# Block 2's modulation with transposed weights, multiplied and summed along the row on VectorE, and no TensorE product

## The chip, the cores and the metric

One core of a Trainium2 chip runs the whole program. The metric is the device time of one launch in microseconds (us), the median over the runs shown. TensorE is called PE below, VectorE DVE, ScalarE ACT and SyncE, which issues nearly all transfers here, SP.

## The reference, cut to what matters

Two transformer blocks run one after the other on 1024 tokens of width 1024. The first ends with an MLP, `h + square(relu(norm(h) @ up_w)) @ down_w`, with a hidden width of 4096. The second is modulated by two small vectors:

```python
mod = silu(c) @ w_ada + b_ada                  # [6*1024]
sh1, sc1, gt1, sh2, sc2, gt2 = split(mod, 6)
mod_c = silu(c_ctx) @ w_ada + b_ada
csh1, csc1, ... = split(mod_c, 6)
hc = rmsnorm(ctx, g_mix) * (1 + csc1) + csh1
h = rmsnorm(x, g_mix) * (1 + sc1) + sh1
...
x = x + gt1 * (mixed @ w_out)
h2 = rmsnorm(x, g_ffn) * (1 + sc2) + sh2
x = x + gt2 * expert_choice_ffn(h2, ...)
```

Only the first two of the six parts are needed for `c_ctx`. So 6144 + 2048 numbers are wanted, each a sum of 1024 products, from a weight matrix of 24 MB. None of them depends on block 1.

## The kernel before

Every large product is made of float32 operands split into a high and a low part: three `pe.matmul` (lines 140 to 142) replace one. Weights come in units of [128, 1024] by a transfer on SP's queue (line 124), ACT writes the high part (115), DVE the low part (116). Five places hold split units, and `wunits` asks for them 1500 instructions ahead of the program's order. The order on each engine is made by a scheduler from the program's order and from when it thinks operands are ready; each engine then runs its queue strictly in order. Memory is 33 places of 4 KB (`R`) and 9 of 2 KB (`T`) per partition; each holds one tile at a time, in program order.

The MLP (755 to 786) runs over nine chunks of the hidden width, of 2, 2 and then 4 blocks of 128 each. In a chunk, "up" makes for each block and each half of the tokens 24 matmuls into one of five PSUM banks (`pm`), ACT takes relu (763) and square (765), DVE writes the two parts of `uT` (767, 768). Then "down" makes 16 groups of matmuls, and DVE adds each to the running sum `acc` (782).

The modulation (722 to 749) is woven into chunks 1 to 6, two of twelve groups of 512 columns in each. At a group, four units of `w_ada` (512 KB each) come into one place, `R32`, one after the other. Each holds two rows-of-128 of the contraction, with the 1024 inputs of the sum on partitions and the 512 outputs along the row. DVE multiplies by the per-partition scalar `cs` (739) and adds the next ones on top (741), into `macc` in place `T4` (and `T5` for `c_ctx`, in the first four groups). The sum over the 128 partitions is a PE product with a column of ones (746). DVE adds the bias `ba`, loaded into `T6` (743), on one partition (748, `mrow` in `T7`), and the row is stored to `mod_d` in DRAM (749). The places T4 to T7 hold before that the tiles `hx` of the residual update `add_out` (622 to 626) at the end of block 1's cross attention. `cs` is one small Silu of ACT (726).

After the MLP, six of the eight rows come back from `mod_d` as columns of 8 floats per partition (803 to 807, `modc`; 1055 to 1058, `modc2`), and enter `to_fm` (210 to 212), `fm_one` (268) and the router's product (1061). Four rows are read back to all partitions (`row_bc`, 791). Block 2 takes place T8 for the table `rope` (833).

Of the kernel before, what the change touches and what calls it, by code (L numbers as in the profile page):

```python
# [34 lines left out]
def tile_kernel(ctx: ExitStack, tc: tile.TileContext, d, out, stop=None, dbg=None):  # L35
# [21 lines left out]
    # On-chip memory: 33 places of 4 KB (R), 9 of 2 KB (T), 3 raw weight units, 5 split  # L57
    # weight units (hi, lo); each place holds one tile at a time, in program order.
# [19 lines left out]
    def tiny(shape, role=None, ring=32):  # L78
        """small vectors: 32 shared places of 8 floats; larger ones in places of their role"""
        n = tn.get(role, 0)  # L80
        tn[role] = n + 1
        return sb.tile(shape, F32, tag=f"y{role or ''}{n % ring}", bufs=1, name=nm("y"))

# [12 lines left out]
    cvec = small[:, 140:156]  # L96
# [8 lines left out]
    def bcast(t, src, n):  # L105
        """t [128, n] <- a row, on every partition"""
        nc.sync.dma_start(t, bass.AP(tensor=src.tensor, offset=src.offset, ap=[[0, 128], [1, n]]))
        return t
# [18 lines left out]
    def wunits(src, i0, n, ahead=1500):  # L127
        """units i0..i0+n of a stream, each [128, 2 (hi, lo), 1024]"""
        res = []
        with tc.high_priority(offset=ahead):  # L130
            for u in range(i0, i0 + n):
                raw = raw_unit(src[u])
                w = sb.tile([128, 2, 1024], F32R, tag=f"W{w_ring[0]()}", bufs=1, name=nm("w"))
                split(w[:, 0, :], w[:, 1, :], raw)
                res.append(w)
        return res

    def mm3(out_, l, r, first, last):
        """l, r: (hi, lo) pairs; out += l.T @ r"""
# [4 lines left out]
    def tm_part(p, lhs, units, k0, first, last):  # L144
        """p[128 tok, 512] += act @ W rows; lhs(k) -> (hi, lo); units: [2k x 512] each, from k0"""
# [9 lines left out]
    def fm_block(p, unit, rhs, n=512):  # L155
        """p[128 m, n tok] = W block.T @ act; unit [8k x 128]"""
# [5 lines left out]
    def rsqrt_of(ss, scale, n=1, eps=EPS):  # L162
        """(ss*scale + eps)^-0.5"""
# [6 lines left out]
        # one Newton step  # L170
# [28 lines left out]
    def evac_split(hi, lo, p, gain=None, shift=None):  # L199
        """hi + lo = p * gain + shift, both per partition"""  # L200
# [16 lines left out]
    def to_fm(xs, regs, banks, name="hT", gain=None, shift=None):  # L217
        """4 token tiles [128 tok, len(regs)*128] -> tiles [128 feat, 2, 512 tok]"""
# [10 lines left out]
    def fm_pairs(xs, regs, banks, gain, shift=None):  # L229
        """2 token tiles -> 4 tiles [128 feat, 2 k, 2 (hi, lo), 256 tok]"""  # L230
# [22 lines left out]
    def fm_one(x, regs, banks, parts=(0, 1), res=None, gain=None, shift=None):  # L253
        """a token tile [128 tok, 1024] -> k -> (hi, lo) [128 feat, 128 tok]"""
# [24 lines left out]
    def tile_of(hT, t):  # L279
        """lhs function of token tile t for hT = {half: [k tiles]}"""  # L280
# [32 lines left out]
    # =========================================================  # L313
    # block 1, mixer
    # =========================================================
# [3 lines left out]
    hT = {}  # L319
# [9 lines left out]
    # positions -> sin, cos [128 tok, 8 tiles, 16]  # L329
# [14 lines left out]
    def turns(k, a, unit):  # L344
        """k <- round(a / (2*pi*unit)) * unit"""
# [24 lines left out]
    # ca, cb -> u  # L370
# [18 lines left out]
    # conv taps  # L389
# [10 lines left out]
    # rg -> silu(rg); q, k rotated  # L400
# [22 lines left out]
    # v  # L423
# [11 lines left out]
    # retention: products in float32, a head's rows apart from the others' by zeros  # L435
# [7 lines left out]
    def retention(t):  # L443
# [7 lines left out]
        # transposes of q0 q1 k0 k1  # L451
# [39 lines left out]
        # state  # L491
# [20 lines left out]
        # group norm  # L512
# [33 lines left out]
    # merged branches, feature-major  # L546
# [43 lines left out]
    # memory keys and values  # L590
# [23 lines left out]
    hxT = Ring([4, 5, 6, 7])  # L614

    def add_out(src, units_src, act_T, tiles, dst_d, name, hxr):
        """dst = src + act @ W for token tiles"""
# [29 lines left out]
    # =========================================================  # L647
    # block 1, cross attention
    # =========================================================
# [65 lines left out]
    # =========================================================  # L715
    # block 1, MLP
    # =========================================================
# [3 lines left out]
    # modulation rows of block 2  # L721
    mod_d = dram([8, 1024], "mod_d")
    ones = cst.tile([128, 1], F32, name="ones")
    dve.memset(ones, 1.0)
    cs = cst.tile([128, 16], F32, name="cs")
    act.activation(cs, cvec, AF.Silu)

    def mod_group(g):
        """512 columns of the modulation"""
        r0, sl = g // 2, slice((g % 2) * 512, (g % 2) * 512 + 512)  # L730
        srcs = [(0, r0)] + ([(8, 6 + r0)] if r0 < 2 else [])
        accs = [T(4 + i, [128, 512], name="macc") for i in range(len(srcs))]
        for c in range(4):
            raw = load(R(32, [128, 1024], name="wada"), d["w_ada"][g * 4 + c]).rearrange("p (j n) -> p j n", j=2)
            for j in range(2):
                k = 2 * c + j
                for (o, _), a in zip(srcs, accs):
                    if k == 0:
                        dve.tensor_scalar(a, raw[:, j, :], cs[:, o:o + 1], None, op0=OP.mult)
                    else:  # L740
                        dve.scalar_tensor_tensor(a, raw[:, j, :], cs[:, o + k:o + k + 1], a, op0=OP.mult, op1=OP.add)  # L741
        ba = T(6, [1, 512], name="ba")
        load(ba, bass.AP(tensor=d["b_ada"].tensor, offset=d["b_ada"].offset + g * 512, ap=[[512, 1], [1, 512]]))
        for (_, r), a in zip(srcs, accs):
            p = B(pt(), "mod")
            pe.matmul(p[:1, :], ones, a, start=True, stop=True)
            row = T(7, [1, 512], name="mrow")
            dve.tensor_add(row, p[:1, :], ba)
            store(mod_d[r:r + 1, sl], row)
# [5 lines left out]
    for ch, fbs in enumerate(MLP_CHUNKS):  # L755
# [28 lines left out]
        if 1 <= ch < 7:  # L784
            mod_group(2 * ch - 2)
            mod_group(2 * ch - 1)

    # =========================================================
    # block 2, mixer
    # =========================================================  # L790
    def row_bc(i, r):
        return bc(i, mod_d[r:r + 1, :])

    def gain_of(i, src, r, tmp):
        """g * (1 + scale)"""
# [6 lines left out]
    modc = cst.tile([128, 4, 8], F32, name="modc")  # L802
    for i, r in enumerate((1, 0, 7, 6)):
        load(modc[:, i, :], mod_d[r:r + 1, :].rearrange("o (k p) -> p (o k)", k=8))
    for i in (0, 2):
        dve.scalar_tensor_tensor(modc[:, i, :], modc[:, i, :], 1.0, g_mix, op0=OP.add, op1=OP.mult)
    a1, sh1, ca1, csh = (modc[:, i, :] for i in range(4))
# [27 lines left out]
    def rotate(dst, p, nh, t):  # L835
        """dst, p: [128, nh*64]; rotation of tile t"""
# [72 lines left out]
    # window attention  # L909
# [21 lines left out]
    def attention(t):  # L931
        qt = load(T(6, [128, 512], name="qt"), q_d[t])
        # per head, partitions: 64 of hi, 64 of lo
# [13 lines left out]
        # keys of the first head of a pair: context, window; of the second: window, context  # L947
        for kv in range(2):
            Pl = []
            for hp in range(2):  # L950
# [3 lines left out]
                for jj in range(2):  # L954
                    h = h0 + jj
                    # context keys end the first bank, window keys start the second
# [9 lines left out]
                    with tc.high_priority(offset=1000):  # L966
                        dve.tensor_reduce(mx, sc, axis=AX.X, op=OP.max)
                        # minus the largest of scores / 8 and sink
# [30 lines left out]
            # rows 0-63: hi part, rows 64-127: correction  # L999
# [10 lines left out]
    # gated short convolution, to DRAM  # L1010
# [39 lines left out]
    # affinities of token tile 4 h + j in columns 32 h.. of part j  # L1050
# [3 lines left out]
    # router on the rows before their norm: logits = rstd * (x @ (gain * w)) + shift @ w  # L1054
    modc2 = cst.tile([128, 2, 8], F32, name="modc2")
    for i, r in enumerate((4, 3)):
        load(modc2[:, i, :], mod_d[r:r + 1, :].rearrange("o (k p) -> p (o k)", k=8))
    dve.scalar_tensor_tensor(modc2[:, 0, :], modc2[:, 0, :], 1.0, g_ffn, op0=OP.add, op1=OP.mult)
    p = B(7, "lb")
    for k in range(8):  # L1060
        pe.matmul(p[:, :16], modc2[:, 1, k:k + 1].to_broadcast([128, 128]), wr[:, k, :], start=(k == 0), stop=(k == 7))
    lbias = cst.tile([128, 16], F32, name="lbias")
    act.activation(lbias, p[:, :16], AF.Copy)
    dve.tensor_mul(wr, wr, modc2[:, 0, :, None].to_broadcast([128, 8, 16]))
# [7 lines left out]
    def mixed(half):  # L1072
        """x += gate * (mixed @ w_out), rows for the experts, affinities"""
# [54 lines left out]
    # =========================================================  # L1128
    # block 2, expert choice
    # =========================================================  # L1130
    # the 128 largest per expert of each half, descending (partitions 0.. and 32..)
# [24 lines left out]
    # slot i: the larger of A[i] and B[127 - i]  # L1156
# [60 lines left out]
    # the last expert's rows by a product with their one-hot matrix, then the norm  # L1217
# [23 lines left out]
def _tm(W, cols):  # L1241
    """column blocks of 512 -> units [128, (2k, 512)]"""
# [16 lines left out]
def _colp(v):  # L1259
    """[n*128] -> [128, n]"""  # L1260
# [37 lines left out]
def layout(inputs):  # L1298
# [8 lines left out]
    small[:, 140:148] = _colp(f["c_2"][0])  # L1307
    small[:, 148:156] = _colp(f["c_ctx_2"])
# [13 lines left out]
    a["b_ada"] = f["b_ada_2"][0]  # L1322
# [15 lines left out]
    # w_ada: 12 column groups x 4 x (2 k)  # L1338
    wa = f["w_ada_2"][0].reshape(4, 2, 128, 12, 512)
    a["w_ada"] = np.ascontiguousarray(np.transpose(wa, (3, 0, 2, 1, 4)).reshape(48, 128, 1024))  # L1340
# [35 lines left out]
```

## Time and profile before

| what | value |
|---|---|
| median of 3 runs | 2591.68 us (2587.64 to 2592.8) |
| span of the profiled execution | 2593.5 us |
| PE busy in the span | 2453.3 us (95%) |
| DVE busy | 1807.0 us (70%) |
| ACT busy | 1155.4 us (45%) |
[...]

The profiled execution is none of the three timed ones. Its span of 2593.5 us, from the first to the last instruction, is the only time given for it, and no time around it is shown. A busy PE is not PE at its peak, since matmuls overlap; what counts is whether it stands idle.

### The profile page before, as it was taken

Reading aid. Unit: us, or ns where it says so; the run is one execution under the profiler, and the core shown is the slowest. Engines: PE = TensorE matmul, PEld = TensorE weight load, DVE = VectorE, ACT = ScalarE, POOL = GpSimd, SP = SyncE. Lnnn points to the kernel's source line nnn. Section 1 sums busy time; section 2 is a strip of 40 time slices with the busy share of each in tenths; the row PEclk is TensorE's granted clock in tenths of the full one; section 3 lists DMA queues with packets and bytes.
Section 4 is the critical chain, followed back from the end, with each engine's and each line's share of the span. In section 5 each row is a group of like instructions: output and inputs, shape, how many; then the busy total and the mean of one; then the engine's idle time right before and its main releaser. Section 6 shows DMA issues by size and latency. Waiting matters only on the chain.

```text
span 2593.5 us, 31426 instructions
## 1 busy us (share of the span) xinstructions
PE 2453.3 (95%) x11504; PEld 1973.3 (76%) x11504; DVE 1807.0 (70%) x3091; ACT 1155.4 (45%) x1773; POOL 54.6 (2%) x35
## 2 busy tenths in 40 slices
PE   7999899999999999999999999999982999999996
PEld 6887678887877877887788777777772888888774
DVE  6999883655566454444434858776557999999888
ACT  6113552545432122112113725554331888887775
POOL 0000000000000000000000000000000100011100
PEclk9999999999999999999999999999995999999998
DMA  5233545334432233223211221114673999999994
GB/s 190 86 122 118 169 165 195 128 108 150 148 121 89 80 94 112 82 82 114 81 49 65 101 83 49 37 54 153 210 280 103 385 394 389 389 388 387 356 355 146
DMA packets 144003, 441.31 MB, mean 170 GB/s; under 512 B 21708, under 2 KB 26316, under 8 KB 143848
## 3 DMA queue, kind: packets, MB, share of 16 engines
q1 hardware_dynamic: 139384, 423.05, 46.1%
q0 software_dynamic: 4464, 16.25, 2.6%
q8 instruction: 90, 1.47, 0.2%
q14 instruction: 65, 0.53, 0.1%
HBM read 387.31 MB, written 51.94 MB: 169 GB/s over the span
## 4 chain that ended last, share of the span: by engine, by line
PE 75%; DVE 11%; DMA 9%; ACT 3%; issue 2%; SPq 0%; ACTq 0%; DVEq 0%; POOLq 0%
PE dn L141 6%; PE dn L142 6%; PE dn L140 6%; PE up L140 5%; PE up L141 5%; PE up L142 5%; DMA h_d<-hx 2%; PE ga L141 2%; PE ga L142 2%; PE wo L140 2%; PE wo L141 2%; PE wo L142 2%; PE ga L140 2%; DMA wada<-w_ada 2%; DVE w L116 2%
## 5 line engine op out<-in xcount | busy, mean ns | idle before, releaser
L115 ACT ACTIVATE w<-raw 128x1024 fp32r<-128x1024 f32 x560 | 584.3, 1058 | 767.6 <-PE dn L142 288.9
L116 DVE TENSOR_TENSOR w<-raw,w 128x1024 fp32r<-128x1024 f32 x560 | 673.7, 1222 | 182.9 <-ACT w L115 177.1
L782 DVE TENSOR_TENSOR acc<-dn,acc 128x512 f32<-128x512 f32 x144 | 98.7, 689 | 154.1 <-PE dn L142 153.9
L140 PE MATMUL up<-hm,w 128*128 128x512 f32 x512 | 201.7, 394 | 0.0
L141 PE MATMUL up<-hm,w 128*128 128x512 f32 x512 | 200.1, 391 | 0.0
L142 PE MATMUL up<-hm,w 128*128 128x512 f32 x512 | 199.9, 390 | 0.0
L140 PE MATMUL dn<-w,uT 128*128 128x512 f32 x512 | 199.4, 389 | 0.1
L141 PE MATMUL dn<-w,uT 128*128 128x512 f32 x512 | 199.2, 389 | 0.0
L142 PE MATMUL dn<-w,uT 128*128 128x512 f32 x512 | 199.0, 389 | 0.0
L396 DVE SCALAR_TENSOR_TENSOR y<-u,small,y 128x1015 f32<-128x1015 f32 (+26 forms) x120 | 146.3, 1262 | 0.6
L140 PEld LDWEIGHTS up<-hm,w 128*128 128x128 f32 x512 | 96.4, 189 | 29.3 <-issue 6.9
L141 PEld LDWEIGHTS up<-hm,w 128*128 128x128 f32 x512 | 96.6, 189 | 20.5 <-issue 0.9
L140 PEld LDWEIGHTS dn<-w,uT 128*128 128x128 f32 x512 | 96.1, 188 | 20.7 <-DVE uT L767 0.5
L142 PEld LDWEIGHTS up<-hm,w 128*128 128x128 f32 x512 | 96.4, 188 | 20.2
L142 PEld LDWEIGHTS dn<-w,uT 128*128 128x128 f32 x512 | 96.1, 188 | 20.1 <-DVE uT L768 0.2
L141 PEld LDWEIGHTS dn<-w,uT 128*128 128x128 f32 x512 | 96.1, 188 | 19.8
L741 DVE SCALAR_TENSOR_TENSOR macc<-wada,cs,macc 128x512 f32<-128x512 f32 x112 | 80.9, 747 | 40.8 <-DMA wada<-w_ada 39.9
L141 PE MATMUL ga<-w,x1T 128*128 128x512 f32 x256 | 102.6, 401 | 1.7 <-DVE w L116 1.7
L141 PE MATMUL dn<-w,x1T 128*128 128x512 f32 x256 | 101.6, 397 | 2.0 <-DVE w L116 2.0
L140 PE MATMUL dn<-w,x1T 128*128 128x512 f32 x256 | 102.4, 401 | 0.0
L142 PE MATMUL ga<-w,x1T 128*128 128x512 f32 x256 | 102.1, 399 | 0.0
L141 PE MATMUL up<-w,x1T 128*128 128x512 f32 x256 | 101.5, 397 | 0.0
(411 smaller groups left out, 5485.6 us busy)
## 6 DMA issues: line engine op xcount, KB each, us to landing
raw<-experts SPq DMA_DIRECT2D x384, 512.0 KB
wada<-w_ada SPq DMA_DIRECT2D x48, 512.0 KB
raw<-up_fm SPq DMA_DIRECT2D x32, 512.0 KB
raw<-down_tm SPq DMA_DIRECT2D x32, 512.0 KB
raw<-w_out_tm SPq DMA_DIRECT2D x24, 512.0 KB
raw<-w_in_fm SPq DMA_DIRECT2D x20, 512.0 KB
h_d<-hx SPq DMA_DIRECT2D x32, 256.0 KB
raw<-xq_fm SPq DMA_DIRECT2D x16, 512.0 KB
```

The lines of the kernel that those rows point to most:

```text
L115: act.activation(hi, src, AF.Copy)
L116: dve.tensor_sub(lo, src, hi.bitcast(F32))
L140: pe.matmul(out_, l[0], r[0], start=first, stop=False)
L141: pe.matmul(out_, l[0], r[1], start=False, stop=False)
L142: pe.matmul(out_, l[1], r[0], start=False, stop=last)
L396: dve.scalar_tensor_tensor(yc[:, s:], uc[:, :1024 - s], convw[:, c, 30 - s:31 - s], yc[:, s:], op0=OP.mult, op1=OP.add)
L741: dve.scalar_tensor_tensor(a, raw[:, j, :], cs[:, o + k:o + k + 1], a, op0=OP.mult, op1=OP.add)
L782: dve.tensor_add(acc[t][:, sl], p, acc[t][:, sl])
```

## The change

The weights are laid out transposed: unit `b` of 48 now holds 128 outputs, one on each partition, with the 1024 weights of each along the row. `silu(c)` and `silu(c_ctx)` lie on every partition as rows, in four tiles of 512 floats. One DVE instruction multiplies 512 weights with 512 inputs and puts their sum in one column. The bias is added as columns, the columns feed block 2 directly, and 32 of them (four rows of the old kind) are transposed by PE, copied and stored in one piece. Comments and docstrings, which make no instruction, are gone as well.

```diff
-    cvec = small[:, 140:156]
...
-    mod_d = dram([8, 1024], "mod_d")
-    ones = cst.tile([128, 1], F32, name="ones")
-    dve.memset(ones, 1.0)
-    cs = cst.tile([128, 16], F32, name="cs")
-    act.activation(cs, cvec, AF.Silu)
-
-    def mod_group(g):
-        """512 columns of the modulation"""
-        r0, sl = g // 2, slice((g % 2) * 512, (g % 2) * 512 + 512)
-        srcs = [(0, r0)] + ([(8, 6 + r0)] if r0 < 2 else [])
-        accs = [T(4 + i, [128, 512], name="macc") for i in range(len(srcs))]
-        for c in range(4):
-            raw = load(R(32, [128, 1024], name="wada"), d["w_ada"][g * 4 + c]).rearrange("p (j n) -> p j n", j=2)
-            for j in range(2):
-                k = 2 * c + j
-                for (o, _), a in zip(srcs, accs):
-                    if k == 0:
-                        dve.tensor_scalar(a, raw[:, j, :], cs[:, o:o + 1], None, op0=OP.mult)
-                    else:
-                        dve.scalar_tensor_tensor(a, raw[:, j, :], cs[:, o + k:o + k + 1], a, op0=OP.mult, op1=OP.add)
-        ba = T(6, [1, 512], name="ba")
-        load(ba, bass.AP(tensor=d["b_ada"].tensor, offset=d["b_ada"].offset + g * 512, ap=[[512, 1], [1, 512]]))
-        for (_, r), a in zip(srcs, accs):
-            p = B(pt(), "mod")
-            pe.matmul(p[:1, :], ones, a, start=True, stop=True)
-            row = T(7, [1, 512], name="mrow")
-            dve.tensor_add(row, p[:1, :], ba)
-            store(mod_d[r:r + 1, sl], row)
+    mod_d = dram([4, 1024], "mod_d")
+    mws = T(8, [128, 512], name="mws")
+    mjunk = mws[:, 0:256].bitcast(BF)
+    mpart = mws[:, 256:384].rearrange("p (h n) -> p h n", h=2)
+    crow = {}
+    for o in range(2):
+        for h in range(2):
+            c = bcast(T(4 + 2 * o + h, [128, 512], name="crow"), d["c_rows"][o, h * 512:(h + 1) * 512], 512)
+            act.activation(c, c, AF.Silu)
+            crow[o, h] = c
+
+    def mod_blocks(b0, n):
+
+        for b in range(b0, b0 + n):
+            raw = load(R(32, [128, 1024], name="wada"), d["w_ada"][b])
+            for o in range(2 if b < 16 else 1):
+                for h in range(2):
+                    dve.tensor_tensor_reduce(out=mjunk, in0=raw[:, h * 512:(h + 1) * 512], in1=crow[o, h],
+                                             op0=OP.mult, op1=OP.add, scale=1.0, scalar=0.0,
+                                             accum_out=mpart[:, h, 48 * o + b:48 * o + b + 1])
...
         if 1 <= ch < 7:
-            mod_group(2 * ch - 2)
-            mod_group(2 * ch - 1)
+            mod_blocks(8 * ch - 8, 8)
...
     def row_bc(i, r):
-        return bc(i, mod_d[r:r + 1, :])
+        return bc(i, mod_d[r - 2:r - 1, :])
...
-    modc = cst.tile([128, 4, 8], F32, name="modc")
-    for i, r in enumerate((1, 0, 7, 6)):
-        load(modc[:, i, :], mod_d[r:r + 1, :].rearrange("o (k p) -> p (o k)", k=8))
-    for i in (0, 2):
-        dve.scalar_tensor_tensor(modc[:, i, :], modc[:, i, :], 1.0, g_mix, op0=OP.add, op1=OP.mult)
-    a1, sh1, ca1, csh = (modc[:, i, :] for i in range(4))
+    modT = cst.tile([128, 64], F32, name="modT")
+    bcol = load(T(5, [128, 64], name="bcol"), d["b_col"])
+    dve.tensor_add(modT, mpart[:, 0, :], mpart[:, 1, :])
+    dve.tensor_add(modT, modT, bcol)
+    a1, ca1, a2c = (cst.tile([128, 8], F32, name=n) for n in ("a1", "ca1", "a2c"))
+    for a, o, g in ((a1, 8, g_mix), (ca1, 56, g_mix), (a2c, 32, g_ffn)):
+        dve.scalar_tensor_tensor(a, modT[:, o:o + 8], 1.0, g, op0=OP.add, op1=OP.mult)
+    sh1, csh, sh2c = modT[:, 0:8], modT[:, 48:56], modT[:, 24:32]
+    p = B(pt(), "modT")
+    pe.transpose(p[:32, 0:128], modT[:, 16:48], ident)
+    mrow = T(6, [32, 128], name="mrow")
+    act.activation(mrow, p[:32, 0:128], AF.Copy)
+    store(mod_d.rearrange("r (k p) -> (r k) p", k=8), mrow)
...
-    modc2 = cst.tile([128, 2, 8], F32, name="modc2")
-    for i, r in enumerate((4, 3)):
-        load(modc2[:, i, :], mod_d[r:r + 1, :].rearrange("o (k p) -> p (o k)", k=8))
-    dve.scalar_tensor_tensor(modc2[:, 0, :], modc2[:, 0, :], 1.0, g_ffn, op0=OP.add, op1=OP.mult)
...
-    a["w_ada"] = np.ascontiguousarray(np.transpose(wa, (3, 0, 2, 1, 4)).reshape(48, 128, 1024))
+    a["w_ada"] = np.ascontiguousarray(f["w_ada_2"][0].T.reshape(48, 128, 1024))
```

The remaining edits put `c_rows` and `b_col` among the inputs in place of `cvec` and `b_ada`, and let the router's product (1061, 1064) read `sh2c` and `a2c` in place of `modc2`.

## Rows read from the trace of the kernel before

**Rows 1.** The page: span, and shares of the chain that ended last by engine.

```profile
span 2593.5 us, 31426 instructions
...
PE 75%; DVE 11%; DMA 9%; ACT 3%; issue 2%; SPq 0%; ACTq 0%; DVEq 0%; POOLq 0%
```

**Rows 2.** Stretches: length, then busy us (count) of PE, PEld, DVE, ACT, POOL; clock.

```profile
760.00:1300.00 540.00, 534.21 (x2310) 428.14 (x2309) 259.47 (x377) 108.81 (x147) 0.00 (x0) 1.00 0.29 89
```

**Rows 3.** All waits of PE from 760 to 1300: total us, times, longest.

```profile
PE mod L746 <- DVE macc L741: 5.8, 6, 1.3
```

**Rows 4.** Same stretch, line 746 alone: length, PE busy, PEld busy.

```profile
760.00:1300.00 540.00, 15.66 (x32) 1.71 (x32) 1.00 0.29 89
```

**Rows 5.** PE in order of time, around one group's product at 1262.

```profile
1261.80 0.39 PE L141 MATMUL dn<-w,uT 128*128 128x512 f32 x1
1262.03 0.39 PE L142 MATMUL dn<-w,uT 128*128 128x512 f32 x1
1262.35 1.02 PE L746 MATMUL mod<-macc,ones 128*1 128x512 f32 x2
1263.30 0.50 PE L140 MATMUL up<-hm,w 128*128 128x512 f32 x1
```

**Rows 6.** Costliest groups of DVE by form, whole span: busy us, mean ns | idle before.

```profile
L741 DVE SCALAR_TENSOR_TENSOR macc<-wada,cs,macc 128x512 f32<-128x512 f32 x112 | 80.9, 747 | 40.8 <-DMA wada<-w_ada 39.9
L768 DVE TENSOR_TENSOR uT<-sq,uT 128x512 fp32r<-128x512 f32 x64 | 44.2, 690 | 1.6
L748 DVE TENSOR_TENSOR mrow<-mod,ba 1x512 f32<-1x512 f32 x16 | 10.8, 676 | 7.8 <-PE mod L746 5.7 <-DMA mod_d<-mrow 2.1
L194 DVE SCALAR_TENSOR_TENSOR x<-x,y,bc 128x1024 f32<-128x1024 f32 x8 | 10.2, 1273 | 0.0
L165 DVE TENSOR_SCALAR y<-y 128x1 f32<-128x1 f32 x68 | 9.9, 148 | 34.4 <-ACT junk L183 34.1
L739 DVE TENSOR_SCALAR macc<-wada,cs 128x512 f32<-128x512 f32 x16 | 7.4, 475 | 17.3 <-DMA wada<-w_ada 10.7 <-DMA h_d<-hx 6.6
```

**Rows 7.** DVE and PE in order of time, end of "up" in one chunk.

```profile
849.79 2.74 DVE L741 SCALAR_TENSOR_TENSOR macc<-wada,cs,macc 128x512 f32<-128x512 f32 x4 [1.31 <-DMA wada<-w_ada]
852.45 0.42 DVE L767 CAST uT<-sq 128x512 fp32r<-128x512 f32 x1
852.90 0.69 DVE L768 TENSOR_TENSOR uT<-sq,uT 128x512 fp32r<-128x512 f32 x1
...
855.30 0.39 PE L140 MATMUL dn<-w,uT 128*128 128x512 f32 x1
```

**Rows 8.** ACT groups by form: table loads, a Silu of 512, the accumulator's read.

```profile
L167 ACT ACT_TABLE_LOAD x18 | 23.1, 1283 | 0.3
L1196 ACT ACTIVATE sa<-ga 128x512 f32<-128x512 f32 x32 | 18.8, 587 | 25.1 <-PE ga L142 25.1
L183 ACT ACTIVATION_READ_ACCUMULATOR junk<-hin 128x1 f32 x16 | 3.1, 196 | 0.0
```

**Rows 9.** The chain of waits, pieces between 690 and 760: start, us, what.

```profile
695.50 4.09 DMA h_d<-hx
...
708.26 4.47 DMA wada<-w_ada
```

**Rows 10.** Waits of all engines, 690 to 760: total us, times, longest.

```profile
DVE macc L739 <- DMA h_d<-hx: 6.6, 2, 5.6
...
PE ptT L223 <- DVE hin L190: 3.9, 1, 3.9
```

**Rows 11.** Tile `modc`: min/median/max ns, first and last start us.

```profile
L210 ACT ACTIVATE mod<-ptT,modc x16: 759/771/788, 1440.9 to 1485.9; 128x512 f32<-128x512 f32 x16
...
L302 SPq DMA_DIRECT2D modc<-mod_d x6: 394/402/509, 837.6 to 1198.3; - x6
```

**Rows 12.** ACT in order of time, its first row.

```profile
0.73 1.28 ACT L726 ACT_TABLE_LOAD   x1 [0.73 <-PEq L1361]
```

**Rows 13.** PE in order of time: one small transpose.

```profile
672.17 0.27 PE L223 MATMUL ptT<-ident,hin 128*128 128x128 f32 x1
```

More of the change, by code (lines that the diff above doesn't have):

```diff
@@ L1053, in tile_kernel @@
     load(wr, d["w_router"].rearrange("p (k e) -> p k e", k=8))
-    modc2 = cst.tile([128, 2, 8], F32, name="modc2")
-    for i, r in enumerate((4, 3)):
-        load(modc2[:, i, :], mod_d[r:r + 1, :].rearrange("o (k p) -> p (o k)", k=8))
-    dve.scalar_tensor_tensor(modc2[:, 0, :], modc2[:, 0, :], 1.0, g_ffn, op0=OP.add, op1=OP.mult)
     p = B(7, "lb")
     for k in range(8):
-        pe.matmul(p[:, :16], modc2[:, 1, k:k + 1].to_broadcast([128, 128]), wr[:, k, :], start=(k == 0), stop=(k == 7))
+        pe.matmul(p[:, :16], sh2c[:, k:k + 1].to_broadcast([128, 128]), wr[:, k, :], start=(k == 0), stop=(k == 7))
     lbias = cst.tile([128, 16], F32, name="lbias")
     act.activation(lbias, p[:, :16], AF.Copy)
-    dve.tensor_mul(wr, wr, modc2[:, 0, :, None].to_broadcast([128, 8, 16]))
+    dve.tensor_mul(wr, wr, a2c[:, :, None].to_broadcast([128, 8, 16]))
     pw = Ring([0, 1, 2, 3])
@@ L1306, in layout @@
     small[:, 128:140] = np.transpose(f["conv_w_2"].reshape(3, 4, 128), (2, 1, 0)).reshape(128, 12)
-    small[:, 140:148] = _colp(f["c_2"][0])
-    small[:, 148:156] = _colp(f["c_ctx_2"])
     for i, n in enumerate(("norm_mix_w", "norm_xattn_w", "norm_mlp_w", "norm_mem_w")):
@@ L1321, in layout @@
     a["ctx"] = f["ctx_2"][0]
-    a["b_ada"] = f["b_ada_2"][0]
+    bcol = _colp(f["b_ada_2"][0])
+    a["b_col"] = np.ascontiguousarray(np.concatenate([bcol, bcol[:, :16]], 1))
+    a["c_rows"] = np.stack([f["c_2"][0], f["c_ctx_2"]])
     W = f["w_in"]
@@ L1337, in layout @@
     a["down_tm"] = np.concatenate(chunks, 0)
-    wa = f["w_ada_2"][0].reshape(4, 2, 128, 12, 512)
-    a["w_ada"] = np.ascontiguousarray(np.transpose(wa, (3, 0, 2, 1, 4)).reshape(48, 128, 1024))
+    a["w_ada"] = np.ascontiguousarray(f["w_ada_2"][0].T.reshape(48, 128, 1024))
     W = f["w_in_2"][0]
```

## The prediction

> **What bounds the kernel now.** I read the shares of the chain that ended last first: PE holds three quarters of it [rows 1]. A mean over the span says nothing of the stage in which the modulation runs, so I then cut out the stretch that holds all of its PE products, 760 to 1300, the middle of the MLP. [...] PE's 5.8 idle microseconds have one cause in the list of waits: the product with ones waits for `macc` [rows 3]. No other instruction of PE waits for anything in these 540 us. So what PE stops doing here comes off the end, as long as nothing new makes it wait. [...]
>
> **The change, part by part.**
>
> *The 16 products with ones go.* In this stretch their 32 instructions (each float32 product is two) cover 15.7 us of PE [rows 4]. The order of time shows that they don't hide beside others: usual matmuls start 0.23 us apart, here the next starts 1.27 us after the last one [rows 5], so one product costs 1.0 us, and 16 some 16 to 17. I take the smaller, 15.7. With them goes the wait of 5.8 us [rows 3], in which the whole "up" stood behind a DVE that itself waited for `w_ada`. Together **-21.5 us**. What is late next is the "up" matmuls themselves, which have their operands.
>
> *DVE's sums change their kind, not their number.* Before: 112 multiply-adds, 16 multiplies and 16 bias additions, 80.9 + 7.4 + 10.8 = 99.1 us [rows 6]. After: 16 blocks of four instructions and 32 of two, so 128 multiply-and-sum instructions on 512 elements. The trace has none. The nearest above it in kind is the multiply-add with two float32 inputs from SBUF, 747 ns; a plain two-input operation takes 690, the lower end [rows 6]. The sum must also be written out: a one-column instruction of DVE takes 148 ns [rows 6], ACT's read of its accumulator 196 [rows 8]. I take 747 + 150 = 0.90 us, an estimate, as this is nearest in operands: 128 x 0.90 = 115 us, 16 more than before. The cover is DVE's 280 idle microseconds [rows 2], so zero. Cover can fail where PE needs `uT` at once, at the end of "up": in one chunk four multiply-adds ran until 852.5, the last needed `uT` was done at 853.6, and PE used it at 855.3, 1.7 us later [rows 7]. Four at 0.90 take 3.6 instead of 2.7 us, 0.9 later, inside that margin: zero again. The upper end is one element in two cycles: 1024 elements take 1273 and 512 take 747 ns, so 512 more steps cost 526 ns [rows 6], 0.75 + 0.53 + 0.20 = 1.47 us each.
>
> [...]
>
> *The 48 loads of `w_ada`* stay: same size, same place R32, and DVE waits for them as before (40.8 us in L741 [rows 6]), now with no PE product behind it.
>
> *The inputs' rows are new*: four broadcasts of 256 KB into T4 to T7, four Silu on ACT. Each waits on SP for the `hx` that held its place to be stored; behind it on SP stand the loads of `hin` and of weights, behind the Silu on ACT the squares of the norm, behind the first sums on DVE the scaling of `hin`, on which PE already waits 3.9 us [rows 10]. Below: `macc` held T4 and T5 early and blocked DVE there for 6.6 us [rows 10]; the new tiles need all four places for a block, and the last is free only after the last `hx`, so DVE may lose this wait and PE its 3.9 us. Above: each fill is a store of 4.1 us, a load (nearest 4.5, twice the bytes) [rows 9], a table load of 1.28 and a Silu of 0.59 [rows 8], 10.5 us; four one after the other in front of the norm make 42, less the 6.6 paid now, 35 us. I take zero: the store is waited for anyway by the `hin` loads, and the rest follows the last `hx` for the reason just given.
>
> *One transpose by PE, two column additions and three gains* take the place of `modc`. The transpose costs 0.27 us [rows 13] and a wait for DVE; I take the mean of the six waits now, 1.0 [rows 3], so **+1.3 us** (ends 0.3 and 1.6). The addition waits on DVE for the load of `bcol`, with `uT` and `acc` behind it; a load of 4.5 us [rows 9] once, in the midst of a chunk, is hidden by PE's PSUM banks.
>
> *Transfers.* SP issues 12 `ba` loads, 16 row stores and 6 column loads fewer, and 4 + 1 + 1 more. The column loads ended 240 us before their first reader [rows 11], so that saves nothing. `rope`, whose place T8 is now held until the sums end, is loaded later, some 150 us before block 2 starts: zero. The first Silu goes from the kernel's start, with a table load of 1.28 us [rows 12]; another function's table may have to come in its place, so zero, or -1.3.
>
> *Sum*: -15.7 - 5.8 + 1.3 = **-20.2 us**. The profiled execution's span is 2593.5 [rows 1], 1.8 above the median of the runs; 2593.5 - 20.2 = 2573.3 there, and 2591.7 - 20.2 = **2571.5** for the median.
>
> **The rivals.**
>
> *Half rate on DVE.* At 1.47 us the four instructions of a block take 5.9 us, 3.1 more than now, and the 1.7 us of margin [rows 7] don't cover that: PE waits 1.4 us at the end of "up", or up to 2.5 more where the load before it takes its longest. That is 3 to 8 us in the two chunks with two outputs; in the four others two instructions add 1.4 us, within the margin unless a load is late too (0 to 2 each). Some 7 us in all: 2578.5. For it: no row shows DVE with two inputs and a running sum at once; against it: L741's rate. Chance 0.10. [...]
>
> *The rows of the inputs hold up the hand-over to the MLP: the slower one.* Its place is 690 to 760, its price up to 35 us as worked out. If two of four fills stand in front of the norm, 21 - 6.6 = 14 us come back: 2586. It decides from 25.4 us on (20.2 gained and 5.2 of 0.2%), that is, if more than three fills are in line before `hin`: up to 2606. For it: the scheduler put `macc` in front of `hx` on DVE, where it waited 5.6 us at once [rows 10]. Against it: the fourth fill cannot stand there. Chance 0.11, of which slower 0.05, no change 0.04.
>
> *Nothing comes off.* PE's freed time is eaten by something that paces the stage as before, such as the weights' split on DVE: 2590. Against it: PE waits for nothing else there [rows 3]. Chance 0.03.
>
> **How the numbers follow.** The forecast has 0.76. A measurement here can tell 0.2%, 5.2 us, from no change. Faster by more: 0.76 + 0.10 + 0.02 = 0.88; within it 0.04 + 0.03 = 0.07; slower 0.05. The range's low end is the forecast with PE's 3.9 us and the table load's 1.3 gained and 2.6 (half the spread of the runs) below: 2563. The high end takes in the half rate and two fills: 2586.
>
> **What would show it.** Right: no PE product in the MLP but one transpose, PE busy all but a microsecond or two of that stretch, the stretch about 20 us shorter, and every later stage as long as before. The new instruction at 0.7 to 1.0 us means full rate; 1.3 or more, with waits of PE for `uT` at the start of "down", the half rate. A wait of PE on `hin` well above 3.9 us before the MLP, with ACT or DVE behind `crow`, means the slower rival. The forecast is wrong if PE has a wait in the MLP that isn't in the list above, or if a later stage grows.

## The result and the profile after

The change made the kernel faster: 2568.48 us median of 4 runs (2567.52 to 2569.4), against 2592.24 us for the kernel before, measured beside it (4 runs, 2587.64 to 2593.1). The ratio is 0.9915, with a 95% interval of 0.9903 to 0.9927. That is 23.8 us less by the medians and 22.0 by the ratio. A later sitting of both kernels, with 15 runs of before, gave 21.4 us less (e7 below). One of its five runs of the changed kernel took 4951.67 us and is left out; 2568.05 us is the median of the other four. Line numbers of the changed kernel are 1 smaller up to the modulation (139 to 141 are the three matmuls), 9 smaller behind it (754 is `relu`, 758 is `uT`).

First the page of the kernel after: its span, the engines' busy time, and the chain that ended last.

```profile
span 2567.6 us, 31478 instructions
...
PE 2433.2 (95%) x11473; PEld 1971.9 (77%) x11473; DVE 1792.5 (70%) x3204; ACT 1164.9 (45%) x1783; POOL 54.5 (2%) x35
...
PE 82%; DVE 8%; DMA 5%; ACT 3%; issue 2%; SPq 0%; ACTq 0%; DVEq 0%; POOLq 0%
```

The chain runs through PE for 82% of the span, before for 75% [rows 1]. In the stretch from 760 to 1300 the chain of before has 9.3% of DMA `wada` and 5.8% of DVE `macc` in it; the chain of after is there PE's matmuls of the MLP alone. The stretch from 760 to 1300, whose row of before is [rows 2], now reads (same columns):

```profile
760.00:1300.00 540.00, 540.00 (x2384) 447.15 (x2383) 256.11 (x495) 113.04 (x153) 0.00 (x0) 1.00 0.30 93
```

PE is busy for all of it, and with 2384 instructions in place of 2310, though 32 of the old ones are gone: 106 more matmuls of the MLP fit in. The list of all waits of PE in the whole MLP of the kernel after, 705 to 1420, has nothing of the modulation (total us, times, longest):

```profile
PE ptT L222 <- DVE hin L189: 3.0, 2, 1.9
PE dn L139 <- ACT relu L754: 1.6, 1, 1.6
PE kv L139 <- DVE hT L210: 0.3, 1, 0.3
PE dn L139 <- DVE uT L758: 0.2, 1, 0.2
PE ptT L222 <- DVE hm L205: 0.2, 1, 0.2
```

The stage's length is read from its first "up" and its last "down" matmul: the views of the tiles `up` and `dn` give the first and the last start of each kind (min/median/max ns ahead of them). Before:

```profile
L140 PE MATMUL up<-hm,w x512: 388/389/774, 709.8 to 1395.7; 128*128 128x512 f32 x171
...
L142 PE MATMUL dn<-w,uT x512: 388/389/486, 727.7 to 1439.6; 128*128 128x512 f32 x171
```

After:

```profile
L139 PE MATMUL up<-hm,w x512: 387/389/496, 707.5 to 1369.7; 128*128 128x512 f32 x171
...
L141 PE MATMUL dn<-w,uT x512: 388/389/421, 723.1 to 1413.7; 128*128 128x512 f32 x171
```

From 709.8 to the last start, 1439.6, before took 729.8 us; after takes 1413.7 - 707.5 = 706.2. Of the 25.9 us between the two spans, 23.6 are in this stage. The 2.3 outside it lie ahead of the stage (its start is 2.3 earlier); from the last "down" matmul to the end both take 1153.9. Far ahead of the stage the change edits only the first Silu and the constant `ones`, though the scheduler's order of PE differs from PE's 33rd matmul on. The four profiles of the two kernels start the stage between 704.3 and 709.8. So the length of this stage is the finer gauge, and it stands below beside each time. It has one weakness: both profiled executions of the kernel before ran long (2595.3 as worked out at the end, and 2595.11 for e0, against medians of 2592.24 and 2589.41), so that a difference from before's MLP may be a microsecond or two too large.

The new instruction, in the view of the tile that takes the sums (median ns in the middle), and what DVE waited for there:

```profile
L738 DVE CUSTOM_DVE_ANT_0 mws<-wada,crow x128: 676/691/695, 705.5 to 1027.3; 128x512 bf16<-128x512 f32 x128
L738 DVE DVE_READ_ACCUMULATOR2_ANT mws<- x128: 77/82/86, 706.1 to 1027.9; 128x1 f32 x128
...
  DMA wada<-w_ada: 101.0, 43
```

A sum costs 0.69 + 0.08 = 0.77 us, and all are done at 1028, 260 us earlier than the last product before (started at 1285). DVE stands 101 us for `w_ada`, more than the 40.8 + 10.7 of before [rows 6], and nobody waits for it. The transpose and its neighbours, in the view of tile `modT`:

```profile
L795 DVE TENSOR_TENSOR modT<-modT,bcol x1: 226/226/226, 1034.1 to 1034.1; 128x64 f32<-128x64 f32 x1
...
L801 PE MATMUL modT<-ident,modT x1: 271/271/271, 1413.9 to 1413.9; 128*32 128x128 f32 x1
...
  DMA bcol<-b_col: 4.3, 1
```

The sums were ready 380 us before PE came to the transpose, which follows the last "down" matmul without a wait. DVE's 4.3 us for `bcol` held up nobody.

### The profile page after: what moved, and what is told of

The parts are those of the page before. It is cut to its first block, busy times and chain, and to the rows that moved or that the text cites. A ratio compares the mean times of both kernels' runs of the same rounds, so it can differ in the third digit from the quotient of the medians.

```text
span 2567.6 us, 31478 instructions
## 1 busy us (share of the span) xinstructions
PE 2433.2 (95%) x11473; PEld 1971.9 (77%) x11473; DVE 1792.5 (70%) x3204; ACT 1164.9 (45%) x1783; POOL 54.5 (2%) x35
## 3 DMA queue, kind: packets, MB, share of 16 engines
q8 instruction: 90, 1.47, 0.2%
## 4 chain that ended last, share of the span: by engine, by line
PE 82%; DVE 8%; DMA 5%; ACT 3%; issue 2%; SPq 0%; ACTq 0%; DVEq 0%; POOLq 0%
PE up L140 7%; PE up L141 7%; PE up L139 7%; PE dn L140 6%; PE dn L141 6%; PE dn L139 6%; PE wo L139 3%; PE wo L140 3%; PE wo L141 3%; PE ga L140 2%; PE ga L141 2%; PE ga L139 2%; DVE w L115 2%; PE q L140 2%; PE q L141 2%
## 5 line engine op out<-in xcount | busy, mean ns | idle before, releaser
L738 DVE CUSTOM_DVE_ANT_0 mws<-wada,crow 128x512 bf16<-128x512 f32 x128 | 88.2, 689 | 103.0 <-DMA wada<-w_ada 101.0
L395 DVE SCALAR_TENSOR_TENSOR y<-u,small,y 128x1007 f32<-128x1007 f32 (+26 forms) x120 | 146.2, 1260 | 0.5
```

What stands on the lines that cost most here:

```text
L395: dve.scalar_tensor_tensor(yc[:, s:], uc[:, :1024 - s], convw[:, c, 30 - s:31 - s], yc[:, s:], op0=OP.mult, op1=OP.add)
L738: dve.tensor_tensor_reduce(out=mjunk, in0=raw[:, h * 512:(h + 1) * 512], in1=crow[o, h], op0=OP.mult, op1=OP.add, scale=1.0, scalar=0.0, a ...
```

## The experiments

My theory: the gain is PE's, the products' own time plus PE's waits for `macc`, and everything put in their place lies beside other work. Rivals: part of the gain is in the hand-over or the transfers; the waits only hide another wait; or DVE's lighter order does it. The experiments remove, put back or double one of these at a time. Two sittings, each with the kernel before measured beside: the first gave 2589.41 us for it (11 runs, 2587.06 to 2591.99), the second 2589.45 (15 runs, 2586.41 to 2594.64); the last experiment had its own (2589.71, 12 runs). MLP is the stage's length as above, in the profiled execution.

| run | time, us | ratio to before, 95% | MLP, us |
|---|---|---|---|
| before, first profile | 2592.24 | | 729.8 |
| e0 before again | 2595.11, one run | | 728.1 |
| after | 2568.48 | 0.9915 (0.9903 to 0.9927) | 706.2 |
| e7 after again | 2568.05 | 0.9915 (0.9899 to 0.993) | 705.0 |
| e1 before without products | 2569.45 | 0.9922 (0.9905 to 0.9938) | 705.8 |
| e2 after, products back | 2583.42 | 0.9973 (0.9963 to 0.9984) | 721.9 |
| e8 before, products of a ready operand | 2584.28 | 0.9973 (0.9963 to 0.9984) | 721.7 |
| e5 before, products of zeros | 2591.54 | 1.0006 (0.9997 to 1.0015) | 721.1 |
| e3 after, sums twice | 2572.39 | 0.9937 (0.9921 to 0.9954) | 711.8 |
| e6 after, no sums | 2572.22 | 0.9933 (0.9917 to 0.9948) | 705.3 |
| e4 after, Silu early | 2577.99 | 0.9956 (0.9943 to 0.997) | 708.7 |

**e0, the kernel before once more**, to see what of its profile recurs: a dip of the granted clock ahead of the stage, and PE's waits.

> The kernel before, unchanged, looked at a second time. The profiles of before and after differ by 23.7 us in the MLP and by 3.8 us in the cross attention ahead of it, where nothing was changed. Theory: the second part is a stop of PE and a dip of the granted clock (0.83 from 600 to 610 us) that before has in every execution, as the order of its queues is fixed; then this profile shows it again and a span of 2592 to 2595. Rival: it belongs to one execution; then PE's stretch from 464 to 655 us is busy at clock 1.00 and the span is 2 to 4 us shorter.

The theory failed: from 600 to 610 us the clock is 1.00 here, so the dip belongs to one execution. The rival's shorter span didn't come either (2593.3 us): other slices have the dip, 310 to 320 with 0.83 among them. PE waited for `macc` 6 times again, 4.3 us in all, at most 1.3, and for `hin` 3.6 us. The MLP took 728.1 us. So the waits that the forecast counted with 5.8 belong to the program; their size varies by a microsecond or two.

**e1, the products away and nothing else.** It leaves out the sum over the partitions: the row is partition 0's sums and the bias.

```diff
-            p = B(pt(), "mod")
-            pe.matmul(p[:1, :], ones, a, start=True, stop=True)
...
-            dve.tensor_add(row, p[:1, :], ba)
+            dve.tensor_add(row, a[:1, :], ba)
```

> Before without the 16 products with ones: the bias is added to the sums of partition 0 alone, so the sum over the 128 partitions is left out. Theory (PE's products and PE's waits for them are the whole gain): 15.7 to 16.7 us of product and 5.8 of wait go, 2570 to 2572, ratio 0.9915 to 0.992, and no wait of PE from 760 to 1300. Rival (the gain comes from the new order of DVE and of the transfers, the other half of the change): under 10 us faster, 2582 or more.

The time fell to 2569.45 us (2565.43 to 2572.78), the MLP to 705.8, which is the changed kernel's. `macc`, its adds, the Silu at the start, 12 `ba` loads, 16 row stores and 6 column loads are all still there, and ahead of the MLP PE's order is that of before, instruction for instruction. So the products with their waits are the whole gain that can be measured; what the other edits are worth together, and the new order with them, is at most 1 to 2 us either way.

**e2, the products put back into the changed kernel**, on a row that is ready before the first sum; nothing reads what they give.

```diff
+    ones = cst.tile([128, 1], F32, name="ones")
+    dve.memset(ones, 1.0)
...
+            if b % 4 == 3:
+                for o in range(2 if b < 16 else 1):
+                    p = B(pt(), "mod")
+                    pe.matmul(p[:1, :], ones, crow[0, 0], start=True, stop=True)
```

> The changed kernel with 16 products with ones put back on PE, at the same places as before, on a row of the inputs that is ready long before, their results unused. Theory: 16 times 1.0 us of PE and no wait, 2568.5 + 16.5 = 2585; what is then missing to before is the wait. Rival (PE has slack here, the products hide beside other work): 2568 to 2572.

The MLP grew from 706.2 and 705.0 to 721.9, by 15.7 to 16.9 us, and the time from 2568.48 and 2568.05 to 2583.42 (2579.57 to 2584.15), by 14.9 to 15.4. PE's and ACT's orders ahead of the MLP are those of the changed kernel. The products' rows in 760 to 1300 (PE's busy time, then PEld's) cover a little less:

```profile
760.00:1300.00 540.00, 14.70 (x32) 2.18 (x32) 0.00 (x0) 0.00 (x0) 1.00 0.29 92
```

A product without a wait costs the stage its 14.70 / 16 = 0.92 us and up to 0.14 more. 6.2 to 7.9 us to before's MLP are still missing: the waits, by the theory.

**e5, the waits away, the products kept** (before; the product reads a tile of zeros, and the row lacks the sum over partitions).

```diff
+    zero = T(8, [128, 512], name="zero")
+    dve.memset(zero, 0.0)
...
-            pe.matmul(p[:1, :], ones, a, start=True, stop=True)
+            pe.matmul(p[:1, :], ones, zero, start=True, stop=True)
...
-            dve.tensor_add(row, p[:1, :], ba)
+            dve.tensor_add(row, a[:1, :], ba)
```

> Before with the 16 products reading a tile of zeros that is ready long before, in place of the sums; their result is not used, and the bias is added to partition 0's sums, so the sum over partitions is left out. Theory (wait and product are two separate terms): the wait of 4.3 to 5.8 us goes, the 15.7 of product stay: 2584 to 2587 where before has 2590. Rival (the waits only move elsewhere, to the next place where PE meets DVE): as before, within 1.5 us.

Here stage and total disagree. The MLP is 721.1 us, 7.0 to 8.7 shorter, as the theory has it; the median time is 2591.54, as before, where the theory had 2584 to 2587. (The profiled execution, 2587.74, is the shortest of the ten; its span of 2585.9 is 7.4 to 7.6 below before's two long ones.) The stretch 345 to 370, 340 us ahead of the edit, shows a loss. In the kernel before, PE's row there (busy, clock) is

```profile
345.00:370.00 25.00, 24.11 (x112) 1.00 0.57 184
```

and in e5

```profile
345.00:370.00 25.00, 20.67 (x94) 0.93 0.51 176
```

with two waits of PE (330 to 370) that before hasn't:

```profile
PE ptz L579 <- DVE z L573: 2.6, 1, 2.6
PE ptz L579 <- ACT zsl L581: 1.6, 1, 1.6
```

The scheduler had put the transposes `ptz` of the merged branches at another place in PE's order, the only difference from before ahead of the MLP. They cost 3.4 us of idle PE and a clock of 0.93 in that stretch, by my estimate 0.07 x 25 = 1.7 us: some 5.2 of the 7.0 to 8.7 us are paid back there. That it is this re-ordering which hides the gain was, with e5 alone, only argued; e8 was made to test it.

**e8, the same without the re-ordering**: the product reads the identity, which lies there from the start, so that no place is taken from another tile. Ahead of the MLP PE's and ACT's orders are those of before, instruction for instruction.

```diff
-            pe.matmul(p[:1, :], ones, a, start=True, stop=True)
+            pe.matmul(p[:1, :], ones, ident[:, None, :].to_broadcast([128, 4, 128]), start=True, stop=True)
...
-            dve.tensor_add(row, p[:1, :], ba)
+            dve.tensor_add(row, a[:1, :], ba)
```

> The kernel before, with its 16 products with ones kept, but their moving operand is the identity, read four times over (512 columns), which lies ready from the start; so PE waits for no sum. The columns that the products give are used by nothing: the bias is added to the row of partition 0 of the sums, so the modulation rows lack the sum over partitions. Unlike in the run with the tile of zeros, no place is taken from another tile, and PE's and ACT's orders ahead of the MLP are as before. My theory (products 15.7 us and waits 4.3 to 5.8 us add up): the MLP takes 722 to 725 us where before took 728.1 and 729.8, no wait of PE on macc, PE's part of 760 to 1300 is 540 of 540, and the time is 4 to 7 us below before's, 2583 to 2586. Rival 1 (the waits are only the last of what would hold PE there anyway, so they come back as another wait): MLP 728 and the time as before, within 2 us. Rival 2 (a product costs more than it covers, so that most of the gain is the products'): MLP 727, time 1 to 3 us below before.

The MLP took 721.7 us, 6.4 to 8.1 below before, and this time the total follows: 2584.28 us (2579.46 to 2584.75), 5.4 below. The stretch 345 to 370 (PE alone) is as before, and PE is busy for all of 760 to 1300 (all engines):

```profile
345.00:370.00 25.00, 24.14 (x117) 1.00 0.55 186
...
760.00:1300.00 540.00, 540.00 (x2346) 435.88 (x2345) 255.40 (x374) 111.93 (x152) 0.00 (x0) 1.00 0.28 89
```

In the MLP's list of waits PE still waits for `hin`, and no longer for a sum:

```profile
PE ptT L223 <- DVE hin L190: 3.4, 1, 3.4
PE dn L140 <- DVE uT L767: 0.4, 1, 0.4
```

e5 has the same products and no waits either, and differs from e8 in the operand and its place T8. Its MLP is 0.6 us shorter, but it starts at 709.6 where e8's starts at 705.0, and its time is 7.3 us longer: the loss lies ahead of the MLP, with the re-ordering.

e8 and e2, the one made from before and the other from after, have the same products and no waits, and the same ratio, 0.9973. The two parts add up: 5.4 us of time for the waits (e8), 14.9 to 15.4 for the products (e2), 20.3 to 20.8 together, where e1 and e7 stand 20.0 and 21.4 below before. That the waits hide another wait is refuted.

**e3, every sum twice**, which adds 128 x 0.77 = 98 us of DVE to the MLP: does DVE's price matter at all?

```diff
-                for h in range(2):
+                for h in (0, 0, 1, 1):
```

> The changed kernel with each of the 128 multiply-and-sums done twice, 98 us more of DVE. Theory (DVE's work is hidden but for the margin of 1.7 us at the end of up): PE waits for uT at the ends of up in the chunks that still run sums, 1 to 5 us each in two to four chunks, so 2570 to 2585. Rival (DVE's time counts in full): 2568 + 98 = 2666. Rival (hidden entirely): 2568.

The MLP took 711.8 us, 5.6 to 6.8 longer, and the time 2572.39 (2571.48 to 2574.09), 3.9 to 4.3 longer. PE loses 2.5 us of 760 to 1300 (second number):

```profile
760.00:1300.00 540.00, 537.46 (x2361) 443.57 (x2360) 334.56 (x735) 111.95 (x152) 0.00 (x0) 1.00 0.29 94
```

and the MLP's waits of PE have

```profile
PE dn L139 <- DVE uT L758: 3.3, 3, 1.9
```

It is the place that the forecast named, the end of "up", where "down" wants `uT` at once [rows 7]. The waits are only half of the loss in this execution: the granted clock is 0.83 in two slices of the MLP, 710 to 720 and 1020 to 1030, each with a stop of PE in it (2.1 us for `hin`, 1.9 for `uT`), by my estimate 0.17 x 10 = 1.7 us each; the changed kernel has 1.00 in every such slice of its MLP. DVE's room is large but not free: at 1.54 us for each sum's place, about the half rate of the first rival (1.47), 4 to 7 us come back, which is near the 7 that the rival was given.

**e6, no sums and no `w_ada` loads** in the changed kernel (the modulation is then that of zeros and the bias): is there anything left to take from them?

```diff
+    dve.memset(mws, 0.0)
...
-            raw = load(R(32, [128, 1024], name="wada"), d["w_ada"][b])
...
+            pass
```

> The changed kernel without the 48 loads of the modulation's weights and without the 128 multiply-and-sums, which leaves the modulation at its bias. Theory (they are wholly hidden behind PE in the MLP): within 1.5 us of the changed kernel. Rival (DVE's 99 us still cost something, at the ends of up or at the hand-over): 3 to 8 us faster than the changed kernel.

The MLP takes 705.3 us, as with them (706.2 and 705.0), though DVE's busy time in 760 to 1300 falls from 256.11 to

```profile
760.00:1300.00 540.00, 540.00 (x2384) 447.26 (x2384) 185.34 (x257) 113.05 (x153) 0.00 (x0) 1.00 0.15 48
```

and the DMA's share by half (0.30 to 0.15). So at 0.77 us the sums and their 24 MB of loads cost nothing in this stage. By time the theory missed: 2572.22 us is 3.7 to 4.2 above the changed kernel's. The stretch 345 to 370 has e5's re-ordering again (20.55 us busy at 0.93, `ptz` waits of 2.6 and 1.8 us), the only difference from the changed kernel in PE's order ahead of the MLP, and the MLP starts 2.6 to 5.8 us later (710.1).

**e4, the Silu of the inputs at the kernel's start**, on 16 x 128 elements, stored and broadcast from there, to take the three table loads out of the hand-over.

```diff
+    cs_d = dram([2, 1024], "cs_d")
+    with tc.high_priority(offset=4000):
+        c_in = load(T(4, [16, 128], name="c_in"), d["c_rows"].rearrange("o (k p) -> (o k) p", p=128))
+        act.activation(c_in, c_in, AF.Silu)
+        store(cs_d.rearrange("o (k p) -> (o k) p", p=128), c_in)
...
-            act.activation(c, c, AF.Silu)
```

> The changed kernel with the Silu of the inputs taken at the start of the kernel on a small tile, stored to DRAM, and broadcast from there; the four Silu of 512 columns and their table loads leave the hand-over to the MLP. Theory (ACT's changes of table delay the norm there, on which PE waits 3.0 and 1.6 us): 1 to 5 us faster than the changed kernel. Rival (the hand-over is paced by the stores and loads of the residual alone): the same within 1.5 us.

A miss: 2577.99 us (2577.05 to 2580.62), slower than the changed kernel, with an MLP of 708.7. The order changed from PE's first dozen instructions on, and the merge of the branches got a wait of its own; the row of 345 to 370:

```profile
345.00:370.00 25.00, 19.01 (x83) 0.86 0.45 149
```

and the wait of PE:

```profile
PE ptz L584 <- DVE z L578: 6.0, 1, 6.0
```

Without the three table loads PE still stood in the hand-over, the longest time for the norm:

```profile
PE ptT L222 <- DVE y L164: 3.6, 1, 3.6
```

So no gain from taking them away is seen. That is as far as the run goes: what the Silu's place alone is worth stays open, since the re-ordering covers it. No version beat the changed kernel.

**e7, the changed kernel again**, in the sitting of e4, e5 and e6.

> The changed kernel again, on the chip of this group, as the base of the others: ratio 0.990 to 0.993 to before, MLP (first matmul of up to last of down) 705 to 708 us.

2568.05 us against 2589.45: 21.4 us less, MLP 705.0.

## Why the prediction was right

The forecast was 2571.5 us and 20.2 us less. The time is 2568.48, inside the range; 21.4 to 23.8 less in the two sittings.

- **The bound.** PE was busy for 534.2 of 540 us at a granted clock of 1.00 [rows 2]. That its time in this stretch comes off the end one for one is what e1, e2 and e8 show, within about 2 us.
- **The products, 15.7.** e2 gives 15.7 to 16.9 in the stage, 14.9 to 15.4 in the time. The forecast saw 16 to 17 in the order of time and took the smaller.
- **The waits, 5.8.** e8 gives 6.4 to 8.1 in the stage, 5.4 in the time. From 760 to 1300 no new wait took their place.
- **The transpose, 1.3: too much.** It costs 0.27, as the row of a small transpose said [rows 13]; the wait of 1.0 that I added didn't come, since the sums end 380 us earlier. I had dated the sums' end by the old pace. In e1 and e8, where no product reads a sum, the old sums too start their last multiply-add at 1011 in place of 1284: it was the tie to PE's products that spread them over the stage.
- **The sums, 0.90 each: too much, with no effect.** They take 0.77: the multiply-and-sum takes 691 ns, about the plain two-input operation's 690, the lower end I named [rows 6], and the accumulator's read takes 82 ns, not 150. Their cost is zero (the MLP takes 705.3 us without them in e6, 706.2 and 705.0 with them). The half rate of the first rival, 1.47 us, was an estimate, and no run shows it: here are two float32 sources from SBUF, a running sum, and 512 elements in 691 ns. The trace calls the instruction CUSTOM_DVE_ANT_0; what a SCALAR_TENSOR_TENSOR with a running sum would take, no run shows.
- **The hand-over, zero.** In the slower rival's place something did move. ACT of the kernel after, in order of time, loads a table for the Silu three times, twice between the squares of the norm and once behind the last:

```profile
703.26 1.28 ACT L729 ACT_TABLE_LOAD   x1
704.55 0.63 ACT L729 ACTIVATE crow<-crow 128x512 f32<-128x512 f32 x1
...
711.52 1.28 ACT L729 ACT_TABLE_LOAD   x1 [0.62 <-DMA crow<-c_rows]
...
726.42 1.28 ACT L729 ACT_TABLE_LOAD   x1
```

But the squares wait for the loads of `hin` anyway. ACT's waits from 690 to 760, of the kernel before and of the kernel after:

```profile
ACT junk L183 <- DMA hin<-h_d: 20.7, 4, 11.8
```

```profile
ACT junk L182 <- DMA hin<-h_d: 17.1, 4, 11.5
```

That idle time is 3.6 us less: the Silu's work lies partly in it. PE's stops in the hand-over add up to 3.0 + 1.6 + 0.2 + 0.2 = 5.0 us in place of 3.9 [rows 10]: 1 us more, and the 1.6 behind `relu` is a wait that the forecast's list didn't have. In e7 it is missing, and the stops add up to 4.0. Against that, before loses some 1.6 us there, by my estimate, at a granted clock of 0.50 for 3.3 us, and the changed kernel, at 1.00, doesn't (last section). The forecast had no term for either, so that they nearly cancel is luck, of 1 to 2 us. The 35 us of the rival needed four fills in line before `hin`. The lower end, a wait of 3.9 us gone, didn't come either.
- **The way from profile to time.** A run's time is its profiled span + 1.8 us (2567.6 and 2569.4). Before's profiled execution was thus 2595.3, 3.1 above its median. The forecast took the span for the time and its 1.8 for the execution's own excess; since the sum was set against the median, nothing followed from it.

## What to carry to other kernels

Here PE was busy for 534.2 of 540 us at a granted clock of 1.00 [rows 2], and 16 small products in its queue cost their length (15.7 us [rows 4]) and the wait for whoever fed them (5.8 us [rows 3]); both could be read beforehand, and 20.0 to 23.8 us came off (e1, e7 and the first runs). The work moved from there onto DVE, busy for 259.47 of the 540 us [rows 2], was free at 0.77 us a sum (MLP of 706.2 and 705.0 us with the sums, 705.3 without), and at twice the sums it delayed `uT`, the one operand that PE wants at once (3.3 us of waits, 3.9 to 4.3 us of time, e3). So read these two numbers, the product's length and its wait, and the margin of that operand, before moving such work. In a kernel whose order a scheduler writes, judge an experiment by the stage it touches and look at the order of the rest: an edit in the MLP re-ordered PE's work 340 us ahead of it, and the time rose by 4 to 7 us (e6 against the changed kernel, e5 against e8).

## What the runs showed of the hardware

Some stops of PE are followed by matmuls at about half pace. In the kernel before, PE in order of time around its wait for `hin` (the wait in brackets):

```profile
716.29 0.39 PE L141 MATMUL up<-hm,w 128*128 128x512 f32 x1
716.52 0.39 PE L142 MATMUL up<-hm,w 128*128 128x512 f32 x1
720.78 0.81 PE L223 MATMUL ptT<-ident,hin 128*128 128x128 f32 x3 [3.87 <-DVE hin L190]
721.24 0.77 PE L140 MATMUL up<-hm,w 128*128 128x512 f32 x1
721.81 0.63 PE L141 MATMUL up<-hm,w 128*128 128x512 f32 x1
722.24 0.63 PE L142 MATMUL up<-hm,w 128*128 128x512 f32 x1
...
723.94 0.58 PE L140 MATMUL up<-hm,w 128*128 128x512 f32 x1
724.36 0.39 PE L141 MATMUL up<-hm,w 128*128 128x512 f32 x1
724.59 0.40 PE L142 MATMUL up<-hm,w 128*128 128x512 f32 x1
```

Matmuls start 0.43 us apart until 724.4 and 0.23 from there on. The granted clock is 0.50 from 721.0 to 724.3, and 0.83 in the slice of 720 to 730. At half the pace for the 3.1 us from 721.2 to 724.4, behind a stop of 3.87, PE loses by my estimate half of them, about 1.6 us. The stops of 3.4 to 3.7 us in e0, e1 and e8 have such a slice too (0.83 to 0.85); the changed kernel, e7 and e2, whose hand-over has stops of at most 2.2, show 1.00. But e3 shows 0.83 with stops of 2.1 at most, and again in the middle of the MLP:

```profile
1023.70 0.50 PE L139 MATMUL dn<-w,uT 128*128 128x512 f32 x1 [1.87 <-DVE uT L758]
...
1025.44 0.63 PE L141 MATMUL dn<-w,uT 128*128 128x512 f32 x1
1025.87 0.63 PE L139 MATMUL dn<-w,uT 128*128 128x512 f32 x1
```

So the length of one stop doesn't decide it alone. Between the two kernels' profiles this is, by the estimate above, some 1.6 us of the MLP's 23.6.

The multiply-and-sum of DVE takes 689 ns in the mean of 128, about as long as a plain two-input operation (690 for `uT` [rows 6]), and its sum comes as a second instruction of 82 ns, less than half of ACT's read of its accumulator, 196 [rows 8].
